# One half's 31-wide convolution as a short Fourier transform on TensorE, and two weight buffers that move into memory the mixer leaves

## The chip, the cores and the metric

The kernel runs on one core of one Trainium2 chip. A core has five engines that each take their own instructions in order: TensorE (PE in the profile; its weight loads are PEld), VectorE (DVE), ScalarE (ACT), GpSimd (POOL) and SyncE (SP), which here only issues DMA transfers. The metric is the device time of one execution in microseconds (us); lower is better. A difference of less than about 0.3% (3.8 us) can't be told from no change by a measurement of this kernel.

## The reference

One layer, on `x` of 1024 tokens by 1024 channels in float32. Its mixer projects the normed tokens, runs an RWKV-7 recurrence on 512 channels and a causal convolution on the other 512, and projects both back; a gated feed-forward network with a 3-wide causal convolution follows. Cut to what matters here:

```python
h = rms_norm(x, norm_pre_mix)
p = h @ w_in
u, q = p[..., :1024], p[..., 1024:]
...                                        # q: RWKV-7 recurrence, group norm, gate -> rwkv_out
c = u[..., :512] * sigmoid(u[..., 512:])
c = causal_dwconv(c, cconv_w, cconv_b)     # 31 taps for each of 512 channels
c = silu(layer_norm(c, cln_g, cln_b))
mix = concatenate([rwkv_out, c], -1) @ w_out
x = x + rms_norm(mix, norm_post_mix)
h = rms_norm(x, norm_pre_ffn)
hid = causal_dwconv(h @ ffn_up, ffn_conv_w, ffn_conv_b)          # 3 taps
gate, up = hid[..., :2816], hid[..., 2816:]
f = (gelu(gate) * up) @ ffn_down
return x + rms_norm(f, norm_post_ffn)
```

## The kernel before

The tokens are worked on in two halves of 512 (h = 0 and 1); the recurrence divides each half into two quarters of 256 (q0 to q3), and a quarter into chunks. Each large product is three matmuls on fp32r operands: a float32 operand is split into a rounded high part and a low remainder (`split`: ACT casts the high part, DVE or POOL subtracts), and high by high, low by high and high by low are added in PSUM. TensorE works through: the projections of half 0, then of half 1; the recurrences of q0 to q2; `w_out(0)`, the output projection of half 0 (768 matmuls of 256 columns in four rounds, with banks `pb`); the norm between mixer and feed-forward for half 0 (`norm_ffn`, tiles `row` and `pt`, which reads the mixer's result back from `mixd` in DRAM); then EARLY = 9 of the feed-forward's up-projections for half 0 (432 matmuls of 512 columns), among which the recurrence of q3 runs; then `w_out(1)`, and the rest of the feed-forward.

The convolution stands beside all this. `conv(h, i)` is, for one block of 128 channels, one ACT instruction (tap 0 and the bias, L428) and 30 DVE SCALAR_TENSOR_TENSOR instructions on 128x512 (L431), accumulating in the PSUM bank `pc`, the last into a tile `co`. `conv_norm(h)` then transposes 128 tokens at a time on TensorE (tiles `co` into `pc`), takes the layer norm over channels on DVE, transposes back (`t2` into `pc`), and applies Silu with gain and bias on ACT (L452). For half 1 the `co` tiles are operands of `w_out(1)`.

Instructions are put in order, per engine, by a scheduler that simulates the program with priorities. A piece of code runs in a "stream" whose number is its priority (`PRIO`, smaller goes first: rwkv 1000, top 100000, norm 200000, conv 300000, proj 400000). `w_out` and the early feed-forward pairs are in "proj", `norm_ffn` of half 0 in "top". `issue_after` gates `conv(1, 0)` and `conv(1, 1)` behind the last Silu of half 0, `conv(1, 2)` behind a mark of q3.

Names used below: `m` are the split operands of `w_out(0)` (L167 is `split`'s subtraction); `mixr` holds the recurrence's results, finished in L774 and L775; `inverses` (L606 and L608, tiles `sub` and `dw`) inverts the small triangular matrices of a quarter by 14 pairs of dependent DVE instructions; `f` are the split operands of the feed-forward (L294); weights are loaded as `wr` and split to `wh` and `wl`, from pool `wp` (3 raw buffers, 2 pairs) and `wq` (2 raw, 1 pair).

## Time and profile before

| | |
|---|---|
| median of 3 runs | 1254.13 us (1252.01 to 1255.34) |
| the profiled execution | 1257.58 us, its span 1255.8 us |
| granted TensorE clock, mean | 0.985 |
| busy: PE, DVE, ACT, POOL | 1210.4, 899.8, 729.1, 507.1 us |

The profiled execution is 3.45 us above the median, and 1.8 us of it lie outside the span. In the profile a line such as L431 is a line of the kernel; `out<-in` gives the tiles by name; "x" counts instructions. A window's columns are the busy us of each engine, then the clock that TensorE was granted (1.00 is full speed), the share of the DMA engines' time, and GB/s. A duration that a record of a matmul shows contains its latency: how fast matmuls follow each other is read from a run of many of them. In the chain of waits, each row is what the engine work was released by, followed back in time.

### The profile page before, as it was taken

How to read it: one execution, taken by the hardware profiler on the slowest of the kernel's cores; microseconds unless marked ns; L12 is line 12 of the kernel's file. 1: busy time of each engine (PE TensorE's matmuls, PEld its weight loads, DVE VectorE, ACT ScalarE, POOL GpSimd, SP SyncE). 2: the span in 40 equal slices, each digit the busy share in tenths (PEclk: the TensorE clock that was granted, in tenths of full speed). 3: DMA queues.
4: the chain of work that ended last, by engine and by line, in shares of the span. 5: the costliest groups of instructions: out<-in, count | busy, mean ns of one | idle time of the engine just before them, and what ended most of it. 6: DMA issues, size and time to landing. Idle time of an engine off the chain costs nothing.

```text
span 1255.8 us, 22979 instructions
## 1 busy us (share of the span) xinstructions
PE 1210.4 (96%) x8424; PEld 988.9 (79%) x8424; DVE 899.8 (72%) x1558; ACT 729.1 (58%) x1515; POOL 507.1 (40%) x447
## 2 busy tenths in 40 slices
PE   5999999999999998999999999999999999999997
PEld 4767777787778876778889888888888888888885
DVE  5285998898669989998640555666656679479667
ACT  7563564565955676466762576876555566554451
POOL 4343330001103331344563399998888850000002
PEclk9999998999999989999999999999999999999999
DMA  7644442333343353222364798894322335336413
GB/s 243 177 131 137 129 135 64 97 128 119 114 128 91 97 178 110 75 80 85 104 186 118 271 323 293 298 315 153 82 74 81 101 134 166 95 117 219 134 52 134
DMA packets 102912, 180.97 MB, mean 144 GB/s; under 512 B 14896, under 2 KB 21424, under 8 KB 102800
## 3 DMA queue, kind: packets, MB, share of 16 engines
q1 hardware_dynamic: 102800, 179.51, 45.6%
q8 instruction: 66, 1.08, 0.4%
q14 instruction: 46, 0.38, 0.1%
HBM read 138.44 MB, written 41.03 MB: 143 GB/s over the span
## 4 chain that ended last, share of the span: by engine, by line
PE 62%; DVE 6%; ACT 2%; issue 1%; DMA 1%; POOL 1%; POOLq 0%; DVEq 0%; ACTq 0%
PE pb L140 27%; PE xs L140 16%; PE pe L140 14%; PE Y L140 2%; PE pc L140 2%; DVE pc L431 2%; DMA pt<-mixd 1%; PE pc L155 1%; PE pe L155 0%; DVE x L1120 0%; DVE m L167 0%; DVE sub L606 0%; DVE nrow L1136 0%; DVE dw L608 0%; DVE t L797 0%
## 5 line engine op out<-in xcount | busy, mean ns | idle before, releaser
L167 POOL TENSOR_TENSOR wl<-wr,wh 128x512 fp32r<-128x512 f32 (+1 forms) x175 | 230.0, 1316 | 219.4 <-ACT wh L167 191.3
L140 PE MATMUL pb<-h,wh 128*128 128x512 f32 (+3 forms) x720 | 230.1, 399 | 2.5 <-ACT wh L167 1.0
L167 ACT CAST wh<-wr 128x512 fp32r<-128x512 f32 (+1 forms) x214 | 131.4, 615 | 131.8 <-issue 42.3
L140 PE MATMUL pb<-f,wh 128*128 128x512 f32 x648 | 205.0, 397 | 2.7 <-ACT wh L167 1.7
L431 DVE SCALAR_TENSOR_TENSOR pc<-c,params,pc 128x512 f32<-128x512 f32 x232 | 174.2, 751 | 8.7 <-ACT pc L428 4.7
L140 PEld LDWEIGHTS pb<-h,wh 128*128 128x128 f32 (+2 forms) x720 | 132.1, 189 | 35.4 <-ACT wh L167 2.7
L140 PE MATMUL pb<-h,wl 128*128 128x512 f32 (+3 forms) x360 | 146.8, 408 | 2.3 <-POOL wl L167 2.1
L140 PEld LDWEIGHTS pb<-f,wh 128*128 128x128 f32 x648 | 121.8, 190 | 28.8 <-ACT wh L167 2.1
L140 PE MATMUL pb<-f,wl 128*128 128x512 f32 x324 | 129.2, 399 | 0.9 <-POOL wl L167 0.9
L162 POOL TENSOR_TENSOR ss<-var,mhalf 128x1 f32<-128x1 f32 x16 | 11.4, 716 | 223.8 <-DVE var L161 223.0
L1076 POOL TENSOR_TENSOR b<-b,b 128x512 f32<-128x512 f32 x72 | 93.3, 1298 | 1.9 <-DMA wr<-ffn_up 0.5
L140 PEld LDWEIGHTS pb<-h,wl 128*128 128x128 f32 (+2 forms) x360 | 67.8, 188 | 20.5 <-POOL wl L167 4.0
L140 PE MATMUL xs<-f,wh 128*128 128x512 f32 x240 | 74.2, 390 | 0.4 <-DVE act L973 0.4
L167 POOL TENSOR_TENSOR wl<-b,wh 128x512 fp32r<-128x512 f32 x48 | 66.6, 1388 | 16.9 <-ACT wh L167 14.9
L140 PEld LDWEIGHTS pb<-f,wl 128*128 128x128 f32 x324 | 61.7, 190 | 14.8 <-POOL wl L167 1.7
L167 ACT CAST wh<-b 128x512 fp32r<-128x512 f32 x48 | 29.7, 618 | 60.0 <-PE pb L140 20.5
L140 PE MATMUL pe<-f,wh 128*128 128x512 f32 x208 | 64.1, 389 | 0.0
L721 POOL TENSOR_TENSOR XG<-r,GE 64x256 f32<-64x256 f32 x30 | 20.5, 683 | 89.3 <-DVE r L740 84.5
L140 PEld LDWEIGHTS xs<-f,wh 128*128 128x128 f32 x240 | 44.9, 188 | 10.0 <-DVE act L973 0.8
L192 ACT CAST wh<-wr 128x512 fp32r<-128x512 f32 (+2 forms) x44 | 26.5, 604 | 44.4 <-PE pb L140 31.2
L167 ACT CAST a<-act 128x512 fp32r<-128x512 f32 x50 | 30.0, 620 | 33.6 <-PE Y L140 19.1
L167 ACT CAST w<-wr 128x512 fp32r<-128x512 f32 x38 | 23.4, 622 | 40.7 <-PE Y L140 20.0
(419 smaller groups left out, 2952.3 us busy)
## 6 DMA issues: line engine op xcount, KB each, us to landing
wr<-ffn_up SPq DMA_DIRECT2D x99, 256.0 KB, 3.2
wr<-w_in SPq DMA_DIRECT2D x80, 256.0 KB, 2.9
b<-ffn_up SPq DMA_DIRECT2D x52, 256.0 KB, 2.7
b<-ffn_down SPq DMA_DIRECT2D x44, 256.0 KB, 4.5
sums<-b SPq DMA_DIRECT2D x44, 256.0 KB, 4.2
wr<-sums SPq DMA_DIRECT2D x44, 256.0 KB, 2.8
lows<-wl SPq DMA_DIRECT2D x40, 256.0 KB, 3.3
wl<-lows SPq DMA_DIRECT2D x40, 256.0 KB, 2.7
```

Of the source, the lines that this page charges most:

```text
L140: return self.nc.tensor.matmul(out, lhsT, rhs, start=start, stop=stop, skip_group_check=skip)
L155: self.nc.tensor.transpose(out, in_, self.con("ident")[:n, :n])
L162: self.nc.gpsimd.tensor_tensor(out, v[:, :n], self.mhalf[:, :n], ALU.pow)
L167: return self.nc.scalar.copy(hi, src), eng.tensor_tensor(lo, src, hi.bitcast(F32), ALU.subtract)
L192: self.nc.scalar.copy(hi, raw)
L431: nc.vector.scalar_tensor_tensor(out, c[:, j:j + HALF], w(j), acc, ALU.mult, ALU.add)
L721: nc.gpsimd.tensor_tensor(x[64:128], R[64:128, gs], w.GE[64:128, c, gs].unsqueeze(2).broadcast_to([64, 4, CH]), ALU.mult)
L1076: sub = lambda o, x, y, op=ALU.subtract: self.nc.gpsimd.tensor_tensor(o, x, y, op)
```

## The change

For half 1, `conv` and `conv_norm` are replaced by `waves`. The 512 tokens, with the 30 before them, are taken in six blocks of SPAN = 116 tokens, of which the last FRESH = 86 are kept (the last block overlaps the fifth). For each block: four transposes put the tokens on partitions (116 tokens by 512 channels, bank `pc`); ACT and DVE split that into `xy`; three matmuls by constant cosines and sines (`wave`) give the spectrum; DVE multiplies it by the taps' spectrum (`tapf`; three multiplications, the last two with halves of the partitions exchanged, and an addition); ACT and DVE split the product into `xy` again; three matmuls transform back to 86 tokens, a last row of `xy` adding the bias; layer norm over the channels on DVE and POOL; four transposes back, and four ACT instructions with gain and bias into `co`. After the sixth block four ACT instructions apply Silu. All blocks use the one bank `pc` and the one `xy`, one after the other. `conv_setup`, once, loads the constants and the taps, splits the constants, and computes `tapf` by two float32 matmuls. The gates of half 1's convolution are gone; `waves(1)` stands in the program behind `w_out(0)`, in stream "proj" ("wave" in PRIO is not used).

The pool `wq` is opened in `setup_ffn`, where the mixer's memory has been given back, and not in `setup`.

Line numbers move: `mm` is L140 before and L162 after, `transpose` L155 and L177, `split`'s subtraction L167 and L189, the inverses L606/L608 and L701/L703, `mixr` L774/L775 and L869/L870.

```diff
+HALO = CONV_W - 1
+SPAN = 116
+FRESH = SPAN - HALO
+NFREQ = SPAN // 2 + 1
...
-        "mixr": 1, "co": 4, "po": 1, "c": 4, "t2": 2}
+        "mixr": 1, "co": 4, "po": 1, "c": 4, "t2": 2, "t3": 2}
...
+def waves():
+    angle = 2 * np.pi / SPAN * (np.arange(SPAN)[:, None] * np.arange(NFREQ)[None, :] % SPAN)
+    cos, sin = np.cos(angle), np.sin(angle)
+    w = np.zeros((P, 3 * P + FRESH), np.float64)
+    w[:SPAN, 0:NFREQ] = cos
+    w[:SPAN, 64:64 + NFREQ] = sin
+    times = np.where(np.arange(NFREQ) % (SPAN // 2) == 0, 1, 2)[:, None] / (2 * SPAN)
+    w[0:NFREQ, P:P + FRESH] = (times * cos.T)[:, :FRESH]
+    w[64:64 + NFREQ, P:P + FRESH] = (times * sin.T)[:, :FRESH]
+    w[P - 1, P:P + FRESH] = 1
+    o = P + FRESH
+    w[:CONV_W, o:o + NFREQ] = w[:CONV_W, o + 64:o + 64 + NFREQ] = cos[:CONV_W]
+    o += P
+    w[:CONV_W, o:o + NFREQ] = -sin[:CONV_W]
+    w[:CONV_W, o + 64:o + 64 + NFREQ] = sin[:CONV_W]
+    return w.astype(np.float32)
+
...
         pool = next(self.homes[tag]) or self.wp
-        bufs = {self.wp: (RAW, PAIRS), self.wq: (MORE_RAW, MORE_PAIRS)}[pool][tag != "wr"]
+        bufs = ((RAW, PAIRS) if pool is self.wp else (MORE_RAW, MORE_PAIRS))[tag != "wr"]
         return pool.tile(shape, dt, tag=tag, bufs=bufs, name=self.nm(tag))
...
         self.wp = ctx.enter_context(tc.tile_pool(name="wp", bufs=1))
-        self.wq = ctx.enter_context(tc.tile_pool(name="wq", bufs=1))
         self.hp = ctx.enter_context(tc.tile_pool(name="hp", bufs=2 * KT))
...
         self.ccarry = cp.tile([P, 4, 32], F32, name="ccarry")[:, :, :CONV_W - 1]
+        self.wave = cp.tile([P, 2, P + FRESH], F32R, name="wave")
+        self.tapf = cp.tile([P, 2, D_CONV], F32, name="tapf")
+        self.xy = cp.tile([P, 2, D_CONV], F32R, name="xy")
...
+
+    def conv_setup(self):
+
+        nc = self.nc
+        raw, tap = (self.tl("ca", [P, 512]) for _ in range(2))
+        nc.sync.dma_start(raw[:, :3 * P + FRESH], self.a["waves"])
+        nc.sync.dma_start(tap[:CONV_W + 1], self.a["taps"])
+        n = P + FRESH
+        nc.scalar.copy(self.wave[:, 0], raw[:, :n])
+        nc.vector.tensor_tensor(self.wave[:, 1], raw[:, :n], self.wave[:, 0].bitcast(F32), ALU.subtract)
+        for e in range(2):
+            ps = self.bank("pc")
+            self.mm(ps, raw[:CONV_W, n + e * P:n + (e + 1) * P], tap[:CONV_W])
+            nc.scalar.copy(self.tapf[:, e], ps)
+        hi, lo = (self.xy[0:32, e] for e in range(2))
+        nc.scalar.copy(hi, tap[0:32])
+        nc.vector.tensor_tensor(lo, tap[0:32], hi.bitcast(F32), ALU.subtract)
+        for e, t in enumerate((hi, lo)):
+            nc.sync.dma_start(self.xy[P - 1:P, e].bitcast(F32), t[CONV_W:].bitcast(F32))
+
+    def waves(self, st):
+
+        nc = self.nc
+        co = [self.tl("co", [P, HALF]) for _ in range(4)]
+        hi, lo = self.xy[:, 0], self.xy[:, 1]
+        n = P - 1
+
+        def product(w, k):
+            ps = self.bank("pc")
+            m = w.shape[2]
+            for i, (a, b) in enumerate(((0, hi), (0, lo), (1, hi))):
+                self.mm(ps[:m], w[:k, a], b[:k], start=i == 0, stop=i == 2)
+            return ps
+
+        def two(k, src):
+            nc.scalar.copy(hi[:k], src[:k])
+            nc.vector.tensor_tensor(lo[:k], src[:k], hi[:k].bitcast(F32), ALU.subtract)
+
+        for b in range(6):
+            t0 = min(b * FRESH, HALF - FRESH)
+            ps = self.bank("pc")
+            for i in range(4):
+                self.transpose(ps[:SPAN, i * P:(i + 1) * P], st["c", i][:, t0:t0 + SPAN])
+            two(SPAN, ps)
+            ps = product(self.wave[:, :, :P], SPAN)
+            y, swap = (self.tl("t3", [P, D_CONV]) for _ in range(2))
+            nc.vector.tensor_tensor(y[:n], ps[:n], self.tapf[:n, 0], ALU.mult)
+            nc.vector.tensor_tensor(swap[0:64], ps[64:128], self.tapf[64:128, 1], ALU.mult)
+            nc.vector.tensor_tensor(swap[64:n], ps[0:n - 64], self.tapf[0:n - 64, 1], ALU.mult)
+            nc.vector.tensor_tensor(y[:n], y[:n], swap[:n], ALU.add)
+            two(n, y)
+            ps = product(self.wave[:, :, P:], P)[:FRESH]
+            bs = self.small.tile([P, 6], F32, tag="cs", name=self.nm("bs"))[:FRESH]
+            nc.vector.bn_stats(bs, ps)
+            mv = self.small.tile([P, 4], F32, tag="cs", name=self.nm("mv"))[:FRESH]
+            nc.vector.bn_aggr(mv[:, 0:2], bs)
+            nc.vector.tensor_scalar(mv[:, 3:4], mv[:, 1:2], 1.0, LN_EPS, ALU.mult, ALU.add)
+            nc.gpsimd.tensor_tensor(mv[:, 2:3], mv[:, 3:4], self.mhalf[:FRESH, 0:1], ALU.pow)
+            xn = self.tl("t3", [P, D_CONV])[:FRESH]
+            nc.vector.tensor_scalar(xn, ps, mv[:, 0:1], mv[:, 2:3], ALU.subtract, ALU.mult)
+            ps = self.bank("pc")
+            for i in range(4):
+                self.transpose(ps[:, i * P:i * P + FRESH], xn[:, i * P:(i + 1) * P], FRESH)
+            for i in range(4):
+                nc.scalar.activation(co[i][:, t0:t0 + FRESH], ps[:, i * P:i * P + FRESH], AF.Identity,
+                                     bias=self.par("cln_b", i), scale=self.par("cln_g", i))
+            yield
+        for i in range(4):
+            nc.scalar.activation(co[i], co[i], AF.Silu)
+            st["co", i] = co[i]
...
         pool = lambda name, bufs=1: ctx.enter_context(tc.tile_pool(name=name, bufs=bufs))
+        self.wq = pool("wq")
         cp = pool("fconst")
...
+        def waves(h):
+
+            with self.stream("proj"):
+                list(self.waves(sts[h]))
+
...
         conv_norm(0)
+        with self.stream("conv"):
+            self.conv_setup()
         project(1, hs, "u0 u1 u2 u3")
...
         step(self.bonus, 2)
-        conv(1, 0, sts[0]["normed"])
-        conv(1, 1, sts[0]["normed"])
         with self.stream("proj"):
             self.w_out(0, mixes[0], [sts[0]["co", i] for i in range(4)])
+        waves(1)
         mixes[1] = self.tl("mixr", [P, 4, HALF])
...
                                ("pb",), dg))
-        conv(1, 2, W[3].mark)
-        conv(1, 3)
-        conv_norm(1)
         with self.stream("proj"):
...
     out["consts"] = constants()
+    out["waves"] = waves()
+    out["taps"] = np.concatenate([f("cconv_w")[0].reshape(CONV_W, D_CONV), f("cconv_b")[0].reshape(1, D_CONV)])
     out["post_mix"] = f("norm_post_mix")
```

Three places in the order of instructions, as built. In a row stand line, operation, output, inputs and shape; a number behind a name is the tile's, and "x3" merges equal rows.

VectorE, at the end of q2's inverses and the first splits `m` for `w_out(0)`. Before, the convolution's L431 stands between nearly all of the steps:

```order
L431 SCALAR_TENSOR_TENSOR pc_703_4615<-c_526_3352,params_78,pc_703_4615 128x512
L606 TENSOR_TENSOR sub_628_4031<-dw_103 128x54
L167 TENSOR_TENSOR m_707_4681<-mixr_338_2009,m_706_4680 128x512
L167 TENSOR_TENSOR m_709_4683<-mixr_338_2009,m_708_4682 128x512
L431 SCALAR_TENSOR_TENSOR pc_703_4615<-c_526_3352,params_78,pc_703_4615 128x512
L608 TENSOR_TENSOR dw_103<-dw_103,sub_628_4031 128x9x6
L382 TENSOR_SCALAR gd_699_4602<-gd_699_4602 96x512
L167 TENSOR_TENSOR m_711_4685<-mixr_338_2009,m_710_4684 128x512
L480 TENSOR_SCALAR kk_640_4066<-pe_641_4073 128x512
L431 SCALAR_TENSOR_TENSOR pc_703_4615<-c_526_3352,params_78,pc_703_4615 128x512
L606 TENSOR_TENSOR sub_629_4034<-dw_103 128x56
```

After, on the same engine and place:

```order
L703 TENSOR_TENSOR dw_100<-dw_100,sub_639_4068 128x2x13
L870 TENSOR_TENSOR mixr_338_2009<-mixr_338_2009,pe_617_3976 128x4x128
L701 TENSOR_TENSOR sub_640_4071<-dw_100 128x14
L703 TENSOR_TENSOR dw_100<-dw_100,sub_640_4071 128x14
L711 STREAM_TRANSPOSE dw_100<-dw_100 64x16x32
L715 STREAM_TRANSPOSE l8_626_4022<-dw_100 64x16x32 x2
L189 TENSOR_TENSOR m_707_4631<-mixr_338_2009,m_706_4630 128x512
L525 TENSOR_TENSOR t3_794_5211<-pc_793_5207,tapf_126 127x512
L526 TENSOR_TENSOR t3_795_5212<-pc_793_5207,tapf_126 64x512
L527 TENSOR_TENSOR t3_795_5212<-pc_793_5207,tapf_126 63x512
```

All of q2's inverses and their last transposes have moved ahead of the first `m`, and a block's spectrum (L525 to L527) stands where L431 stood.

TensorE, at the first matmuls of the feed-forward (`pb` from `f`). Before:

```order
L155 MATMUL xs0_100<-const_79,v_662_4403 64x128 x2
L140 MATMUL pe_831_5506<-pt_645_4218,const_79 128x512
L140 MATMUL pe_832_5509<-pt_655_4318,const_79 128x512
L140 MATMUL pb_899_6087<-kk_856_5937,row_888_6028 128x128
L140 MATMUL pb_899_6087<-kk_856_5937,row_892_6044 128x128
L140 MATMUL pb_899_6087<-kk_856_5937,row_888_6028 128x128
L140 MATMUL pb_899_6087<-kk_856_5937,row_892_6044 128x128
L155 MATMUL xs1_101<-const_79,v_677_4484 64x128 x2
L140 MATMUL pb_929_6255<-f_868_5976,wh_931_6258 128x512
```

After:

```order
L162 MATMUL xs1_98<-r_901_6027,ck_867_5629 64x64
L162 MATMUL Y_102<-r_901_6027,ca_851_5504 64x64
L162 MATMUL xs1_98<-r_901_6027,ck_867_5629 64x64
L162 MATMUL Y_102<-r_901_6027,ca_851_5504 64x64
L162 MATMUL pc_823_5339<-xy_127,wave_125 86x512 x3
L162 MATMUL pb_959_6295<-f_926_6174,wh_961_6298 128x512
L162 MATMUL pb_959_6295<-f_927_6175,wh_961_6298 128x512
```

The last matmuls of a half's norm are no longer next to the feed-forward's first: chunk matmuls of the recurrence and the fourth block's inverse transform stand directly ahead of it.

TensorE, at the last matmuls for half 1's convolution, amid the 432 of the early feed-forward. Before, the last transposes back (`t2` into `pc`) stand behind 396 of them:

```order
L140 MATMUL pb_1061_6955<-f_875_5983,wh_1063_6958 128x512
L140 MATMUL pb_1061_6955<-f_874_5982,wl_1064_6959 128x512
L155 MATMUL pc_927_6245<-const_79,t2_926_6243 128x128 x4
L140 MATMUL pb_1061_6955<-f_876_5984,wh_1066_6976 128x512
L140 MATMUL pb_1061_6955<-f_877_5985,wh_1066_6976 128x512
```

After, the last block's transposes back (`t3` into `pc`) stand behind 193:

```order
L162 MATMUL pb_1016_6599<-f_940_6188,wl_1022_6621 128x512
L162 MATMUL pb_1025_6645<-f_926_6174,wh_1027_6648 128x512
L177 MATMUL pc_845_5431<-const_76,t3_844_5429 128x86 x4
L162 MATMUL pb_1025_6645<-f_927_6175,wh_1027_6648 128x512
L162 MATMUL pb_1025_6645<-f_926_6174,wl_1028_6649 128x512
```

They have moved forward by about four of the nine feed-forward pairs, and none of the convolution's work is left near `w_out(1)`.

2 lines of the change are left out of this document (1 added, 1 removed).

## The prediction

> **What bounds the kernel now.** I read the page first: engines, chain, groups.
>
> ```profile
> span 1255.8 us, 22979 instructions
> PE 1210.4 (96%) x8424; PEld 988.9 (79%) x8424; DVE 899.8 (72%) x1558; ACT 729.1 (58%) x1515; POOL 507.1 (40%) x447
> PE 62%; DVE 6%; ACT 2%; issue 1%; DMA 1%; POOL 1%; POOLq 0%; DVEq 0%; ACTq 0%
> L431 DVE SCALAR_TENSOR_TENSOR pc<-c,params,pc 128x512 f32<-128x512 f32 x232 | 174.2, 751 | 8.7 <-ACT pc L428 4.7
> ```
>
> TensorE bounds most of the span. The removed work (half of L431) is on VectorE, which the chain visits for 6%. So the change pays only where VectorE stops TensorE. The busy time by stage tells where:
>
> ```profile
> 390.00:411.00 21.00, 20.76 (x155) 19.53 (x154) 21.00 (x43) 10.68 (x25) 6.54 (x5) 0.92 0.31 88
> 411.00:457.00 46.00, 44.61 (x724) 41.19 (x724) 43.37 (x69) 33.85 (x76) 16.59 (x15) 1.00 0.43 119
> 457.00:500.00 43.00, 36.50 (x449) 27.53 (x442) 36.24 (x87) 29.17 (x76) 10.60 (x14) 0.92 0.43 144
> 500.00:560.00 60.00, 59.57 (x700) 47.56 (x701) 56.30 (x93) 33.44 (x69) 24.51 (x20) 0.97 0.26 76
> 560.00:633.00 73.00, 72.91 (x534) 58.82 (x532) 56.57 (x92) 48.28 (x102) 33.87 (x28) 1.00 0.31 93
> 633.00:641.00 8.00, 5.38 (x19) 4.05 (x19) 5.30 (x6) 6.13 (x12) 5.04 (x5) 0.79 0.49 146
> 641.00:700.00 59.00, 58.64 (x438) 56.17 (x437) 8.22 (x13) 19.22 (x53) 26.15 (x21) 1.00 0.50 145
> 700.00:1250.00 550.00, 546.27 (x2425) 451.78 (x2423) 375.84 (x600) 320.66 (x657) 287.86 (x228) 1.00 0.53 170
> ```
>
> From 390 to 457 both are full (VectorE 21.0 of 21.0, 43.4 of 46.0). A busy PE is not PE at its peak there, since latencies of small dependent matmuls count. From 641 on TensorE is dense and VectorE has nothing of the convolution: that part stays. Its order is the same in both kernels from `w_out(1)` on, so the whole result is decided by when `w_out(1)` begins. The chain of waits gives the stage borders:
>
> ```profile
> 388.85 0.60 DVE mixr L775
> 413.67 0.18 DVE dw L608
> 470.06 4.17 DMA pt<-mixd
> 500.38 10.71 PE pb L140 x46
> 636.39 15.67 PE pb L140 x106
> 652.05 11.52 PE xs L140 x96
> 773.37 10.88 PE pb L140 x48
> ```
>
> And from TensorE's and VectorE's timelines:
>
> ```profile
> 389.50 1.09 PE L155 MATMUL pe<-const,l 128*128 128x128 f32 x8 [2.19 <-DVE mixr L775]
> 390.35 0.36 PE L140 MATMUL pb<-wh,m 128*128 128x256 f32 x1
> 456.54 0.28 PE L140 MATMUL pb<-wh,m 128*128 128x256 f32 x1
> 634.74 0.73 PE L140 MATMUL pb<-f,wh 128*128 128x512 f32 x2 [1.70 <-ACT wh L167]
> 636.39 0.50 PE L140 MATMUL pb<-f,wl 128*128 128x512 f32 x1 [0.92 <-POOL wl L167]
> 379.15 0.17 DVE L606 TENSOR_TENSOR sub<-dw 128x14 f32<-128x14 f32 x1
> 493.76 0.18 DVE L606 TENSOR_TENSOR sub<-dw 128x14 f32<-128x14 f32 x1
> 508.19 0.17 DVE L608 TENSOR_TENSOR dw<-dw,sub 128x14 f32<-128x14 f32 x1
> ```
>
> Stage A, `w_out(0)`, runs from 390.4 to 456.8: 66.4 us. Stage B, the norm, ends with the first feed-forward matmul at 500.4: 43.6. Stage C, early feed-forward and q3, ends with the first matmul of `w_out(1)`. Its first 96 matmuls of 256 columns end at 652.05 and take 11.52 us by the next 96, so it begins at 640.5: C is 140.1. Behind it lie 615.3 us to the end. A 512-column matmul streams at 10.88/48 = 0.227 us, a 256-column one at 0.120.
>
> The convolution slows the chain in A, where by VectorE's groups it takes half of the engine's time (first row, 390 to 457; the second is of stage B):
>
> ```profile
> L431 DVE SCALAR_TENSOR_TENSOR pc<-c,params,pc 128x512 f32<-128x512 f32 x44 | 32.9, 748 | 0.4
> L555 DVE TENSOR_TENSOR l<-pe,const 128x256 f32<-128x256 f32 x8 | 3.3, 416 | 0.1
> ```
>
> Therefore q2's inverses take 379.15 to 413.85 between L431s, 34.7 us; q3's, with few of them, 493.76 to 508.36, 14.6.
>
> **The change, part by part.** The `pc` tile view prices the old instructions:
>
> ```profile
> L431 DVE SCALAR_TENSOR_TENSOR pc<-c,params,pc x232: 723/756/757, 134.5 to 583.2; 128x512 f32<-128x512 f32 x116
> L155 PE MATMUL pc<-const,t x32: 270/273/328, 318.6 to 627.0; 128*128 128x128 f32 x32
> L452 ACT ACTIVATE co<-pc,params x32: 447/458/466, 322.1 to 631.1; 128x128 f32<-128x128 f32 x32
> L428 ACT ACTIVATE pc<-c,params x8: 772/780/785, 133.7 to 543.1; 128x512 f32<-128x512 f32 x8
> L447 DVE TENSOR_SCALAR t<-pc,mv x8: 800/810/811, 315.4 to 624.0; 128x512 f32<-128x512 f32 x8
> 391.71 1.28 DVE L167 TENSOR_TENSOR m<-mixr,m 128x512 fp32r<-128x512 f32 x2
> 496.78 1.88 PE L140 MATMUL pe<-pt,const 128*128 128x512 f32 x4
> 511.02 2.20 PE L140 MATMUL pe<-dw,l 32*32 32x16 f32 x128
> ```
>
> *VectorE* loses 120 x 0.75 = 90 us of L431 and 4 x 1.9 of norm (two passes over 512 of at most L447's 0.81, two tiny ones) = 7. Each of six blocks adds two splits (2 x 0.64), three multiplications from PSUM and one addition (between a split's 0.64 and L447's 0.81: 3.0), statistics and norm (1.8): 6.1, together 36. Net -61 us.
>
> *ScalarE* loses 4 x 0.78 and 16 x 0.46 = 10.4; gains per block two casts (bounded by L428's 0.78; about 0.62) and four of at most 0.46: 3.0, and four final Silu of about 0.7: +21. Net +10, on an engine that is 58% busy; no wait of it is on the path except at the tail below.
>
> *TensorE* gains 36 matmuls of 512 columns, 8.2 us, and loses 32 transposes of 128 columns for 48 shorter ones, +1.0 (eight transposes take 1.09 us in the 389.50 row, 0.11 to 0.12 each behind the first; the 273 ns is latency; 86 columns I take at 0.08). Two float32 512-column products cost 1.88 by the 496.78 row (four pieces there). Sum +11, and all of it is on the engine that bounds. This is the price against the gain.
>
> *Set-up* (two loads and two row copies on SP's queue, six splits and copies) comes at about 240 us, among loads that wait for free buffers in the same way. SP would hold the following weight loads if a `ca` buffer came late; bounds 0 to some 3 us (a load's landing), I take 0: whatever TensorE loses ahead of 389 is covered, since it waits there 2.19 us for `mixr`, a VectorE result. The 2.5 us that set-up and the first block put on TensorE before `w_out(0)` are hidden there too.
>
> *The weight buffers.* The first two loads into `wq` stand amid `w_out(1)`'s in both orders, and after the change they have no wait on the mixer. Cost 0; if they had, one late weight costs about what the tail shows now, 1.7 + 0.9 us, plus the clock.
>
> *Where the work moves, by the order.* Priced with the rates above, and the small ones by the pace of their streams (2.20/128 us a record in the 511.02 row, up to 0.06 for 64 columns by estimate), TensorE's own work is, before and after: A 58.6 and 71.0; B 26.4 and 30.4; C 123.0 and 115.2. The freed VectorE lets the scheduler pull q2's chunk products and scores into A (+8.6 of the 12.4; blocks are the rest), and q3's inverses and their matmuls into B.
>
> Start of A: ahead of the first `m`, VectorE sheds about fifteen L431 (10 us), but now does all the rest of q2's inverses and three transposes there (about 9). So `m` is ready when it was: start 390.
>
> A: 71.0 of work, 1.7 for the half-clock stretch (below), and 2.3 of waits, where 66.4 - 58.6 - 1.7 = 6.1 are now. VectorE sheds 33 us of L431 here and takes on some 20 (a block and a half, q3's scores), so its waits shorten; the blocks bring their own chain through one bank, so they don't vanish. 75.0, +8.6.
>
> B: a chain, not an engine, sets it (PE work 26.4 of 43.6): results to DRAM and back (4.17 for a tile), `row`, `pt`, `f`. VectorE is busy 36.2 of 43 now. By the order q3's scores, which L555 stands for, leave it for A (L555 3.3, L556, L564 and L597 with it; some 11 us), and two blocks (12 us) and the rest of q3's inverses (up to 14.6 less what waits there, some 6 by the 0.18 rows) enter. Above, that makes 43.6 + 12 = 55.6 if the blocks stand wholly on the chain; below, 40 if what leaves is on the chain and what enters fits into waits such as the 4.17. I take 45.6, +2.0, near to now, since what leaves and what enters differ by only 7 us and the norm's own `row` steps keep their places.
>
> C: 115.2 of work. Of the 17.1 us above the work now, 2.6 are the two gaps at 634.74 and 636.39, where TensorE waits for weights that ACT and POOL split late behind the convolution's norm, and 3.4 two half-clock stretches. The tail's two go: the last block now ends half a stage earlier. The other 11.1 are the mixing of small dependent matmuls with feed-forward; a third of those matmuls left, and the last 48.6 us are feed-forward alone, so I take 6. 115.2 + 1.7 + 6 = 122.9, -17.2. What is late next at the tail: nothing of the mixer; weights, at their present pace.
>
> Sum: +8.6 + 2.0 - 17.2 = -6.6. Against the profiled 1257.58 that is 1251.0; against the median, 3.45 lower, 1247.5.
>
> **The clock.** Three stretches ran at half speed:
>
> ```profile
> 391.20:394.60 3.40, 3.40 (x11) 2.37 (x12) 3.40 (x8) 3.40 (x8) 0.00 (x0) 0.50 0.00 0
> 459.50:466.30 6.80, 6.66 (x52) 3.71 (x52) 2.99 (x7) 4.68 (x15) 1.40 (x2) 0.50 0.90 287
> 637.00:640.40 3.40, 3.40 (x10) 2.63 (x9) 1.30 (x2) 1.98 (x3) 2.27 (x2) 0.50 0.61 176
> ```
>
> Each 3.4 us cost 1.7. The last follows gaps of 1.70 and 0.92 us, so removing the tail's stall also removes 1.7. The Trainium skill (TensorE: Matmul & The Clock Gate, "HAM oscillation") has the rule that idle gaps of TensorE over about 3.4 us matter; by it the tail's short gaps cost no clock, and the sum would be -4.9. The trace disagrees: its gaps are shorter, and the clock fell. The same page (Part 4) says that transposes on TensorE don't count as busy for the gate; with more of them and of small matmuls in A and B, one more half-clock stretch would follow, and the sum by it would be -4.9 too. No run here shows that alone.
>
> **Rivals.**
> 1. *The norm becomes VectorE's* (slower). Blocks and q3's inverses stand between the norm's own `row` and `f` instructions, in order. For: 36.2 of 43 us busy there already, and the first feed-forward matmul has a block's inverse transform ahead of it on TensorE, so it waits for that block's VectorE work. Against: q3's scores leave. At B = 56, the upper end, the sum is +3.8, the point from which it is slower; with half the inverses besides (63), +11. About 1259.
> 2. *No change.* The pulled-forward work saves nothing since it was dense where it was: waits stay 6.1 in A, and 9 in C: -6.6 + 3.8 + 3 = about 0: 1254. For: VectorE's share of the chain is 6%. Against: 34.7 us for inverses that take 14.6.
> 3. *More gain.* With VectorE free, A is as dense as its work (72.7), B is 40, C 120: 6.3 - 3.6 - 20.1 = -17: about 1237. For: TensorE's work in the three rises 8.6 us, and 42 us of them are not its work now (66.4 + 43.6 + 140.1 less 208.0).
> 4. *The buffers' move delays the feed-forward's weights*: +4. Against: no wait in the order.
>
> **How the numbers follow.** The forecast has 0.50, its own range 1242.5 to 1252.5; 0.39 of it is faster by over 0.3% (3.8 us; below 1250.4), 0.11 within. Rival 1: 0.20, slower. Rival 2: 0.15, of which 0.12 is within and 0.03 slower. Rival 3: 0.13, faster. Rival 4: 0.02, within, as it takes most of the gain back. Faster 0.55, same 0.25, slower 0.20. The range 1238 to 1259 leaves out nearly half of rival 1 and most of rival 3, 2 in 10.
>
> **What would show it.** Right: L431 x116; `w_out(0)` from 390 to about 465; the first feed-forward matmul near 511; first matmul of `w_out(1)` near 634 with no gap on `wh` and `wl` ahead and no half clock; 615 us behind it. Wrong: B over 55 us with VectorE over 95% busy and TensorE idle on `f` or `pc` (rival 1); `w_out(1)` at 640 with C at 128 (rival 2); `w_out(0)` ending by 463 and B at 40 (rival 3); a `wr` from `ffn_up` that lands late in `w_out(1)` (rival 4). The sum fails most easily in B, the stage with no bound from its own work.

## The result, and the profile after

The changed kernel takes 1270.37 us (median of 5 runs, 1267.52 to 1273.3) against 1254.65 before (5 runs): ratio 1.0135, 95% interval 1.0122 to 1.0147. It is 16 us slower, where 6.6 us faster had been forecast. The page of its profile:

```profile
span 1270.8 us, 23041 instructions
PE 1222.7 (96%) x8480; PEld 999.5 (79%) x8480; DVE 846.3 (67%) x1484; ACT 734.3 (58%) x1535; POOL 504.5 (40%) x449
L455 DVE SCALAR_TENSOR_TENSOR pc<-c,params,pc 128x512 f32<-128x512 f32 x116 | 87.1, 751 | 3.4 <-ACT pc L452 0.9
```

The change did what it says: half of the convolution's instructions are gone (x116), and VectorE is busy 53.5 us less. TensorE is busy 12.3 us more. The three stages, with borders read as in the prediction, and two stretches inside the second (windows: PE, PEld, DVE, ACT, POOL busy, then the clock):

```profile
391.50:474.70 83.20, 81.38 (x1096) 73.12 (x1095) 51.85 (x90) 52.66 (x121) 27.78 (x26) 1.00 0.34 104
474.70:527.30 52.60, 43.38 (x746) 35.70 (x745) 41.40 (x101) 37.69 (x93) 9.38 (x14) 0.77 0.29 94
527.30:654.50 127.20, 123.19 (x766) 98.59 (x765) 73.08 (x110) 73.73 (x157) 59.20 (x48) 1.00 0.31 94
487.10:490.50 3.40, 3.40 (x49) 2.62 (x49) 3.29 (x8) 2.43 (x7) 0.13 (x1) 0.50 0.38 140
493.90:514.40 20.50, 16.06 (x310) 14.41 (x311) 15.56 (x36) 11.77 (x29) 4.87 (x7) 0.50 0.38 130
```

| | start of A | A, `w_out(0)` | B, norm | C, early feed-forward | from `w_out(1)` on |
|---|---|---|---|---|---|
| before | 390.4 | 66.4 | 43.6 | 140.1 | 615.3 |
| forecast | 390 | 75.0 | 45.6 | 122.9 | 615.3 |
| after | 391.5 | 83.2 | 52.6 | 127.2 | 616.3 |

C did shrink, by 12.9 us, and the tail's stall is gone. A and B grew by 16.8 and 9.0 us, about twice what C gave back. In B the trace shows how TensorE is held up. TensorE's timeline (a bracket is the idle time ahead of a row, and what ended it):

```profile
486.64 1.32 PE L162 MATMUL pc<-xy,wave 116*128 116x512 f32 x3
492.89 0.46 PE L162 MATMUL pc<-xy,wave 128*86 128x512 f32 x1 [1.66 <-ACT xy L514]
496.62 1.16 PE L162 MATMUL pc<-xy,wave 128*86 128x512 f32 x2 [3.27 <-DVE xy L515]
504.87 2.93 PE L162 MATMUL pb<-kk,row 128*128 128x128 f32 x12 [1.72 <-DVE mv L535]
...
526.51 0.94 PE L162 MATMUL pc<-xy,wave 128*86 128x512 f32 x3
527.29 0.62 PE L162 MATMUL pb<-f,wh 128*128 128x512 f32 x2
...
654.45 1.72 PE L162 MATMUL pb<-wm,l 128*128 128x256 f32 x13
```

and VectorE's, at the longest of these waits:

```profile
491.45 0.68 DVE L528 TENSOR_TENSOR t<-t,t 127x512 f32<-127x512 f32 x1
...
493.15 0.75 DVE L982 SCALAR_TENSOR_TENSOR row<-pt,nr,row 128x512 f32<-128x512 f32 x1 [0.88 <-DMA pt<-mixd]
493.82 0.17 DVE L703 TENSOR_TENSOR dw<-dw,sub 128x14 f32<-128x14 f32 x1
495.21 0.75 DVE L982 SCALAR_TENSOR_TENSOR row<-pt,nr,row 128x512 f32<-128x512 f32 x1 [1.22 <-DMA pt<-mixd]
495.88 0.68 DVE L515 TENSOR_TENSOR xy<-t,xy 127x512 fp32r<-127x512 f32 x1
```

A block's inverse transform waits on TensorE, 1.66 and 3.27 us, for the split L514 and L515 of its spectrum. The low part's L515 had its operands early: L514 was done at 492.8. But it is queued behind two `row` steps of the norm, for which VectorE waits 0.88 and 1.22 us on DMA transfers. So the block waits for the norm's DMA, and everything behind the block in TensorE's queue, the norm's matmuls of `kk` and `row` among it, waits for the block: the in-order queues hold each other up. Those matmuls later wait 1.72 us more, put down to a tiny step of a block's norm (L535) that ran among the norm's own. TensorE's clock is at half for 20.5 us meanwhile (493.9 to 514.4).

### The profile page after: what moved, and what is told of

Read it like the earlier page. It is cut to its first block, busy times and chain, and to the rows that moved or that the text cites. A ratio compares the mean times of both kernels' runs of the same rounds, so it can differ in the third digit from the quotient of the medians.

```text
span 1270.8 us, 23041 instructions
## 1 busy us (share of the span) xinstructions
PE 1222.7 (96%) x8480; PEld 999.5 (79%) x8480; DVE 846.3 (67%) x1484; ACT 734.3 (58%) x1535; POOL 504.5 (40%) x449
## 4 chain that ended last, share of the span: by engine, by line
PE 50%; DVE 1%; DMA 0%; POOL 0%; issue 0%; DVEq 0%; POOLq 0%; ACT 0%
PE pb L162 19%; PE xs L162 15%; PE pe L162 12%; PE Y L162 2%; PE pc L162 2%; DVE x L1216 0%; DVE nrow L1232 0%; DMA mixd<-t 0%; PE pc L177 0%; PE Y L177 0%; POOL ss L184 0%; DVE t L892 0%; DVE act L1069 0%; DVEq L1579 0%; POOLq L1579 0%
## 5 line engine op out<-in xcount | busy, mean ns | idle before, releaser
L189 POOL TENSOR_TENSOR wl<-wr,wh 128x512 fp32r<-128x512 f32 (+1 forms) x175 | 227.9, 1304 | 228.3 <-ACT wh L189 185.0
L162 PE MATMUL pb<-h,wh 128*128 128x512 f32 (+3 forms) x720 | 230.4, 399 | 2.5 <-ACT wh L189 1.0
L162 PE MATMUL pb<-f,wh 128*128 128x512 f32 x648 | 202.1, 392 | 3.0 <-ACT wh L189 1.5
L189 ACT CAST wh<-wr 128x512 fp32r<-128x512 f32 (+1 forms) x214 | 131.3, 615 | 126.7 <-issue 41.4
L162 PEld LDWEIGHTS pb<-h,wh 128*128 128x128 f32 (+2 forms) x720 | 131.9, 189 | 35.9 <-ACT wh L189 2.7
L162 PE MATMUL pb<-h,wl 128*128 128x512 f32 (+3 forms) x360 | 146.8, 408 | 2.3 <-POOL wl L189 2.2
L162 PEld LDWEIGHTS pb<-f,wh 128*128 128x128 f32 x648 | 121.0, 188 | 29.3 <-ACT wh L189 2.3
L162 PE MATMUL pb<-f,wl 128*128 128x512 f32 x324 | 127.5, 394 | 0.6 <-POOL wl L189 0.6
L455 DVE SCALAR_TENSOR_TENSOR pc<-c,params,pc 128x512 f32<-128x512 f32 x116 | 87.1, 751 | 3.4 <-ACT pc L452 0.9
L162 PEld LDWEIGHTS pb<-h,wl 128*128 128x128 f32 (+2 forms) x360 | 67.7, 188 | 20.9 <-POOL wl L189 4.0
L162 PE MATMUL xs<-f,wh 128*128 128x512 f32 x240 | 74.2, 390 | 1.4 <-DVE act L1069 1.4
L189 POOL TENSOR_TENSOR wl<-b,wh 128x512 fp32r<-128x512 f32 x48 | 65.5, 1366 | 19.6 <-ACT wh L189 17.9
L162 PEld LDWEIGHTS pb<-f,wl 128*128 128x128 f32 x324 | 60.8, 188 | 14.1 <-POOL wl L189 1.4
L189 ACT CAST wh<-b 128x512 fp32r<-128x512 f32 x48 | 29.7, 618 | 59.8 <-PE pb L162 21.2
L162 PE MATMUL pe<-f,wh 128*128 128x512 f32 x208 | 64.1, 389 | 0.0
L162 PEld LDWEIGHTS xs<-f,wh 128*128 128x128 f32 x240 | 44.9, 188 | 11.1 <-DVE act L1069 1.8
L1015 DVE SCALAR_TENSOR_TENSOR pt<-pb,params,pt 128x511 f32<-128x511 f32 (+1 forms) x36 | 26.9, 747 | 34.8 <-ACT ecarry L1008 34.2
L189 ACT CAST a<-act 128x512 fp32r<-128x512 f32 x50 | 30.0, 619 | 33.6 <-PE Y L162 19.1
```

The source lines that it names most:

```text
L162: return self.nc.tensor.matmul(out, lhsT, rhs, start=start, stop=stop, skip_group_check=skip)
L189: return self.nc.scalar.copy(hi, src), eng.tensor_tensor(lo, src, hi.bitcast(F32), ALU.subtract)
L455: nc.vector.scalar_tensor_tensor(out, c[:, j:j + HALF], w(j), acc, ALU.mult, ALU.add)
L1015: nc.vector.scalar_tensor_tensor(acc[:, o:], ps[:, :HALF - o], w(j), acc[:, o:], ALU.mult, ALU.add)
```

## The experiments

Each is compared with runs of the kernel before on the same chip. "Rows" are the TensorE rows of the recurrence that the order puts into A, B and C (before: 262, 208, 420; after: 376, 354, 164). Stages are those of one profiled run each. e1's and those of the kernel before have the same matmuls, within the few records that a trace lacks, and differ by up to 2.1 us (C), so a smaller difference of one stage says little by itself. e2, e7, e9 and e13 to e18 leave out work of half 1's convolution and compute something else there.

| | median us | ratio, 95% interval | start, A, B, C, rest |
|---|---|---|---|
| e1 buffers only | 1253.37 | 0.9992, 0.9981 to 1.0004 | 389.9, 65.7, 42.3, 138.0, 615.5 |
| e2 two taps | 1258.68 | 1.0040, 1.0025 to 1.0055 | 387.7, 78.5, 42.7, 132.5, 615.4 |
| e3 blocks behind norm | 1274.24 | 1.0154, 1.0128 to 1.0180 | 390.1, 76.5, 44.2, 136.0, 626.3 |
| e4 36 matmuls more | 1259.58 | 1.0041, 1.0027 to 1.0055 | 390.3, 66.2, 41.5, 144.2, 615.6 |
| e5 before, `w_out(0)` first | 1274.04 | 1.0157, 1.0121 to 1.0192 | 390.6, 56.9, 61.3, 146.9, 616.7 |
| e6 after, `w_out(0)` first | 1279.21 | 1.0197, 1.0167 to 1.0226 | 391.5, 63.3, 60.2, 144.2, 616.8 |
| e7 two taps, `w_out(0)` first | 1270.75 | 1.0130, 1.0094 to 1.0166 | 386.5, 63.0, 51.6, 148.8, 615.4 |
| e8 after, blocks first too | 1279.85 | 1.0204, 1.0173 to 1.0236 | 390.5, 64.2, 64.9, 139.0, 618.5 |
| e9 two taps, recurrence held | 1254.24 | 1.0001, 0.9986 to 1.0016 | 386.8, 69.4, 42.6, 137.7, 615.6 |
| e10 after, recurrence held | 1271.38 | 1.0130, 1.0095 to 1.0164 | 391.4, 71.2, 53.5, 138.5, 616.7 |
| e11 e10, five blocks behind the norm | 1274.48 | 1.0158, 1.0119 to 1.0196 | 390.5, 69.3, 46.5, 147.8, 618.4 |
| e12 after, 24 matmuls fewer | 1271.38 | 1.0136, 1.0111 to 1.0160 | 391.4, 87.4, 51.2, 123.4, 615.4 |
| e13 after, no product | 1270.51 | 1.0128, 1.0107 to 1.0149 | 389.7, 82.2, 45.2, 132.6, 618.4 |
| e14 e9 and set-up | 1257.32 | 1.0034, 1.0021 to 1.0046 | 388.2, 68.4, 42.3, 139.4, 616.8 |
| e15 e14 and TensorE's work | 1261.36 | 1.0058, 1.0042 to 1.0074 | 389.4, 68.8, 43.6, 142.9, 616.8 |
| e16 e14 and the steps | 1271.63 | 1.0133, 1.0108 to 1.0158 | 388.3, 76.9, 46.9, 141.0, 616.0 |
| e17 e14, work and steps | 1267.83 | 1.0107, 1.0079 to 1.0135 | 388.3, 77.9, 44.9, 138.2, 616.3 |
| e18 e12 and e13 together | 1263.26 | 1.0059, 1.0041 to 1.0077 | 389.6, 79.2, 48.1, 129.7, 615.3 |

**The parts of the change, one at a time.** The buffers alone:

```diff
-        self.wq = ctx.enter_context(tc.tile_pool(name="wq", bufs=1))    # setup
+        self.wq = pool("wq")                                            # setup_ffn
```

> The kernel before with only the pool wq moved into setup_ffn. Theory 1 (work: each microsecond that the blocks and the tap spectra add to TensorE is paid, wherever they stand) and theory 2 (place: the blocks cost because they and the chunks pulled forward stand in w_out(0) and in the norm): no change, 1254 to 1255. Rival: the buffers' move itself delays loads, then 3 us or more of the 16 are here.

No change; this part of the prediction holds. The relief of VectorE alone:

```diff
-        for j in range(1, CONV_W):
+        for j in range(first, CONV_W):          # first = CONV_W - 1 for half 1
```

> The kernel before, with half 1's convolution cut to its first and last tap (116 of 120 VectorE instructions of it left out, so it computes another convolution there); its norm and transposes stay, and nothing is added. It is the relief of VectorE alone. By the prediction's reasoning (waits in w_out(0), mixing among the early feed-forward and the tail's stall come from VectorE's queue): 15 us or more faster, 1235 to 1240. Theory 1: TensorE was idle only 11 us in these stages and at half clock for 17 us; VectorE is behind a part of that, so 4 to 8 us faster, 1247 to 1251. Theory 2 says the same of the relief as long as the chunks it pulls forward do no harm; if they do (the order is looser and the norm gets longer), no gain or a loss, 1253 to 1262.

With 87 us less for VectorE and nothing more for any engine, the kernel is slower, by 0.40%, where the prediction's reasoning asks for 15 us or more the other way; theory 2's 1253 to 1262 holds. This was the run that overturned the forecast. Its stages:

```profile
387.70:466.20 78.50, 76.07 (x1047) 68.67 (x1044) 42.10 (x73) 49.59 (x114) 25.06 (x23) 1.00 0.38 114
466.20:508.90 42.70, 31.05 (x567) 26.06 (x565) 36.04 (x93) 28.19 (x68) 10.70 (x14) 0.92 0.34 115
508.90:641.40 132.50, 129.45 (x952) 103.63 (x950) 64.26 (x100) 81.56 (x171) 62.30 (x49) 0.99 0.31 90
```

A is 12 us longer, since the scheduler pulls chunks forward (rows 360, 274, 260). C gives back 7.6, and the norm keeps its 43 us with TensorE less busy in it (31.05 us; 36.5 of 43 before). Blocks out of the norm, and their TensorE work as idle repeats in the kernel before:

```diff
-        waves(1)                                # behind w_out(0)
+        with tc.issue_after(self.mark_lo.ins):  # behind norm_ffn(0)
+            waves(1)
```

> The changed kernel, with the six blocks gated behind half 0's norm, so that all of them stand among the early feed-forward. Theory 1: their matmuls cost the same there, 1264 to 1268 (only the norm's extra idle time of some 3 us comes back). Theory 2: the norm falls back to 44 us, its half-clock stretch of 20 us goes, w_out(0) ends earlier; 1250 to 1257.

B fell to 44.2, as theory 2 says, but the time didn't: the last block came so late that `w_out(1)` waited for it (5.70 us at 672.41, for the split of a `co`), and the rest grew by 11. Both theories missed. Inconclusive on the work.

```diff
+                for _ in range(extra if first else 0):      # 2 for the nine early pairs
+                    self.mm(ps[:m], wh[:, kk], hi)
```

> The kernel before, with two idle repeats of the first matmul of each up-projection in the nine early pairs: 36 matmuls of 512 columns more (the number that the blocks add), and nothing else. Theory 1: 36 x 0.227 = 8.2 us slower, 1262 to 1263. If TensorE has slack there that they fill (what the prediction called mixing), less: 1256 to 1259.

36 matmuls cost 5.1 us (interval 3.4 to 6.9), less than their 8.2 at 0.227, and between the two expectations. Added work is paid for the most part.

**Giving the recurrence another place.** e2 suggested a third theory, that the norm is a chain of fixed length in which chunk products are free. Four runs put `w_out(0)` ahead of the recurrence:

```diff
+PRIO = {"out": 500, ...}
-        with self.stream("proj"):
+        with self.stream("out"):
             self.w_out(0, ...)
```

> The kernel before, with w_out(0) in a stream of its own, ahead of the recurrence (number 500, rwkv has 1000): q2's chunk products leave w_out(0) for the norm and the early feed-forward (262 matmul rows of the recurrence in w_out(0) before, 105 here). Theory 3, formed from the runs so far: the norm is a chain of some 43 us whatever TensorE does in it, so chunk products are free there and are paid in w_out(0) and among the feed-forward; freeing VectorE only made the scheduler pull them into w_out(0). By it w_out(0) falls to about 59, the norm stays at 44, the early feed-forward grows to about 146: 1250 to 1255. Rival (theory 1: work is work wherever it stands): no change, 1254.

> The changed kernel, with w_out(0) in the same stream ahead of the recurrence (376 matmul rows of the recurrence in w_out(0) after the change, 164 here). Theory 3: w_out(0) about 64 instead of 83, the norm about 48 (it keeps blocks), the early feed-forward about 141; 1255 to 1261, so most of the 16 us come back. Theory 1: the blocks' work is paid all the same: 1264 or more.

> The kernel before with half 1's convolution cut to two taps (116 VectorE instructions left out), and w_out(0) ahead of the recurrence. Theory 3: the relief is worth something only so: w_out(0) 61, norm 43, early feed-forward 141; 1246 to 1251, against 1258.7 with the relief alone. Theory 1: TensorE's work is that of the kernel before, so 1252 to 1255. If the relief itself did the harm and not the pulled-forward chunks: 1257 or more.

> The changed kernel, with w_out(0) and the six blocks in the stream ahead of the recurrence: the blocks end after 96 of the 432 early matmuls, and 34 of their TensorE rows stand in the norm. Theory 3: w_out(0) about 64, and the norm as after or longer, since more blocks' chains stand on TensorE's queue in it (50 to 55): 1257 to 1264. Theory 1: 1264 or more.

Theory 3 missed all four, by 16 to 20 us. Theory 1's "1264 or more" held for e6 and e8, its 1254 for e5 did not, so moving the recurrence costs by itself. A shrank as expected (56.9 in e5), but the norm is no free room. Its stages in e5, the kernel before with only this edit:

```profile
390.60:447.50 56.90, 55.66 (x588) 52.70 (x586) 51.84 (x88) 27.53 (x61) 21.72 (x18) 0.98 0.36 102
447.50:508.80 61.30, 49.05 (x660) 39.43 (x659) 43.03 (x91) 41.30 (x105) 9.28 (x13) 0.72 0.38 123
508.80:655.70 146.90, 142.10 (x1309) 111.59 (x1310) 124.52 (x200) 88.74 (x183) 63.83 (x54) 0.99 0.28 84
```

With the chunks in it B is 61.3 us at a clock of 0.72. The third theory fell: B does not get shorter with less in it, but longer with more.

So the next runs held how much of the recurrence stands in each stage. Putting only the first two of `w_out(0)`'s four rounds ahead gives rows 266, 208, 420, nearly those of the kernel before:

```diff
+            with self.stream("out") if h == 0 and ch in (0, 1) else ExitStack():
+                round(ch)
```

> The kernel before with half 1's convolution cut to two taps (116 VectorE instructions left out) and only the first two of w_out(0)'s four rounds ahead of the recurrence. That puts as much of the recurrence into each stage as the kernel before has (matmul rows of it in w_out(0), norm, early feed-forward: 266, 208, 420; before 262, 208, 420; with the relief alone 360, 274, 260). Theory 4, from the runs so far: the norm's chain has a floor of some 42 us; less TensorE work than fits into it is idle time there, more (or work in long dependent chains at half clock) lengthens it, and the kernel before happens to stand at the best filling. By it the relief at this filling is a small gain: 1247 to 1253 (tail and waits in w_out(0)), against 1258.7 for the relief with chunks pulled forward. Rival: VectorE's instructions do no harm where they were, and the loss of the relief had another cause: 1255 or more.

```profile
386.80:456.20 69.40, 66.45 (x863) 60.97 (x860) 34.69 (x51) 44.36 (x100) 23.64 (x21) 1.00 0.39 109
456.20:498.80 42.60, 35.88 (x455) 27.18 (x453) 36.00 (x87) 29.39 (x76) 9.98 (x14) 0.96 0.44 146
498.80:636.50 137.70, 135.36 (x1245) 107.53 (x1246) 70.96 (x128) 87.39 (x177) 61.47 (x51) 1.00 0.29 87
```

Theory 4's gain did not come; the time is that of the kernel before, 1.0001. VectorE is busy 34.7 us in A, where it was 64.4 of 67 from 390 to 457, and q2's inverses end at 388.95 instead of 413.85. `w_out(0)` starts 3.6 us earlier, since TensorE's wait of 2.19 us for `mixr` is gone, but A is 3.0 us longer and ends where it did (456.2; 456.8 before). A wait as long has come up on another tile (first row TensorE, the others VectorE):

```profile
393.79 0.39 PE L140 MATMUL pb<-wh,m 128*128 128x256 f32 x1 [2.21 <-DVE gd L365]
388.79 0.16 DVE L608 TENSOR_TENSOR dw<-dw,sub 128x14 f32<-128x14 f32 x1
389.58 1.13 DVE L616 STREAM_TRANSPOSE dw<-dw 64x512 f32<-64x512 f32 x1
390.73 2.10 DVE L620 STREAM_TRANSPOSE l<-dw 64x512 f32<-64x512 f32 x2
392.99 0.74 DVE L365 SCALAR_TENSOR_TENSOR gd<-pb,params,gd 96x511 f32<-96x511 f32 x1
```

L365 empties a bank `pb`, and is queued behind the transposes that follow the inverses. The tail's two gaps are gone too, but C's 137.7 is no shorter than the 138.0 of e1, which has the same gaps (1.70 and 0.92 us) and a whole convolution. So the relief moved waits and brought no time. Two limits: e9 holds the recurrence's share of each stage, not the order itself, and the first two rounds put ahead without the cut were not run, so it is not shown that this edit costs nothing alone.

> The changed kernel with only the first two of w_out(0)'s rounds ahead of the recurrence: the recurrence is distributed as before (266, 208, 420 matmul rows), and the blocks stand as after (a block and a half in w_out(0), two in the norm, the rest behind it). Theory 4: the pulled-forward chunks' share comes back, the blocks' own work (8 to 9 us) and their stalls in the norm (6 to 9 us) stay: 1261 to 1267. If the chunks pulled forward are not part of the loss: 1270.

> As the last, with only the first block free to run in w_out(0) and the other five gated behind half 0's norm, so that no block stands in the norm and the last ends behind 374 of the 432 early matmuls. Theory 4: the norm is back at 42 to 44, w_out(0) at 67 to 69, the early feed-forward at 143 to 147 with five blocks' work: 1256 to 1261, so that only the blocks' TensorE work is left of the loss. If the blocks' stalls on TensorE cost as much among the feed-forward as in the norm: 1264 or more.

Theory 4 missed both; the other expectation, 1270 for e10 and 1264 or more for e11, held in both. Holding the recurrence shortens A by 12 us and lengthens C by 11. With one block early and five behind the norm (`next(blocks)` once, the others gated), B comes down to 46.5, and C goes up to 147.8, 10 us over e9's with the same matmuls of recurrence and feed-forward. Of these 10, five blocks' 30 matmuls are 6.8 at 0.227. The blocks' cost moves with them.

**Work or chains.** The changed kernel with fewer matmuls, with a shorter chain, and with both:

```diff
-            for i, (a, b) in enumerate(((0, hi), (0, lo), (1, hi))):      # e12, e18
-                self.mm(ps[:m], w[:k, a], b[:k], start=i == 0, stop=i == 2)
+            self.mm(ps[:m], w[:k, 0], hi[:k])
...
-            nc.vector.tensor_tensor(y[:n], ps[:n], self.tapf[:n, 0], ALU.mult)   # e13, e18: all four gone
-            two(n, y)
+            two(n, ps)
```

> The changed kernel with one matmul in place of three in each of the blocks' transforms (high part by high part only, so the convolution is less exact): 24 matmuls of 512 columns, 5.4 us of TensorE, are gone; VectorE's and ScalarE's steps stay. Theory 1 (the loss is TensorE's added work): 1264 to 1266. Theory 5 (the loss is the blocks' chains, in which TensorE's in-order queue stands still): no change, 1269 to 1271.

> The changed kernel without the multiplication by the taps' spectrum (three multiplications and one addition on VectorE, 3 us of each block's chain, are left out, so that no convolution is computed); all of TensorE's work stays. Theory 1: no change, 1268 to 1271. Theory 5: the chain is shorter by six times 3 us, of which the two to four blocks that TensorE waits for come back: 1260 to 1265.

> The changed kernel with both cuts: one matmul of three, and no multiplication by the taps' spectrum. The recurrence then stands as in the first two-tap run (360, 274, 260 matmul rows in the three stages; that was 1258.7). Theory 1: 1264 to 1266. Theory 5: 1260 to 1266, as chains are shorter and fewer of them stand in the norm. If neither work nor chain length matters, only that blocks stand in TensorE's queue at all: 1268 to 1271.

Neither edit alone moved the time, as theory 5 had it for e12 and theory 1 for e13; neither theory has both. The two together took the ratio from 1.0135 to 1.0059, within theory 5's range. In e13 the norm did fall, to 45.2, and C and the rest rose by 7.5. The order is made anew for each kernel, and gives one stage what another saves; effects do not add. The other way round, on top of e9, the change was built up piece by piece:

```diff
+            self.conv_setup()                   # e14 to e17
+            self.work(sts[1])                   # e15, e17: 36 matmuls, 16 transposes into pc, constant operands
+            self.steps(sts[1])                  # e16, e17: casts, subtractions, products, norms in SBUF
```

> The kernel of the two-tap run with the held distribution (1254.2), and conv_setup (loads, splits, two float32 matmuls) besides, whose results are not used, with wq moved to make room. Prediction's pricing: hidden ahead of w_out(0), 1254. Theory 1: its 1.9 us of TensorE and some 2 us by which w_out(0) begins later in all kernels that have it: 1256 to 1258.

> The last kernel, with the blocks' TensorE work besides, without their chains: six times three 512-column matmuls by the cosines and three by the inverse, on constant operands, and 16 transposes, into the bank pc, with nobody waiting for the results; no VectorE or ScalarE step of a block. TensorE then has as much work as in the changed kernel. Theory 1: 1264 to 1269. Theory 5: work without chains fills TensorE's idle time in the norm, 1256 to 1261, and the rest of the loss up to 1270 is the chains.

> The set-up run (1257.3) and the blocks' VectorE and ScalarE steps besides, on other data in memory and with no TensorE work: six times two casts, two subtractions, three multiplications and one addition, and for two blocks the norm (the other four norms stand for those of the old code, which stays). Results unused. Theory 5 (the loss beyond set-up and work is the waits between the engines): 1256 to 1259, since VectorE and ScalarE are not the bound. Rival: these steps hold up the norm's and the recurrence's on their in-order engines: 1262 or more.

> The work-alone run (1261.4) with the same steps besides: as much work on every engine as in the changed kernel, but the blocks' matmuls don't wait for the steps, nor the steps for them. Theory 5: 1261 to 1264, and the 7 to 9 us up to the changed kernel are the waits between matmuls and steps. Rival (load on VectorE and ScalarE): 1267 or more.

Against the kernel before: relief 0.0%, with set-up 0.34%, with TensorE's work 0.58%, with work and steps 1.07%, the change 1.35%. In e15 the norm takes up the extra matmuls (TensorE busy 40.9 of 43.6, clock 1.00, where e9 has 35.9), much as theory 5 had it, though 1261.36 lies just above its range:

```profile
389.40:458.20 68.80, 68.02 (x875) 62.37 (x873) 29.70 (x47) 43.98 (x99) 24.11 (x21) 1.00 0.39 113
458.20:501.80 43.60, 40.90 (x491) 31.13 (x489) 35.34 (x90) 29.98 (x76) 8.50 (x13) 1.00 0.41 136
501.80:644.70 142.90, 137.35 (x1254) 110.47 (x1249) 75.97 (x125) 87.86 (x180) 63.11 (x52) 0.98 0.29 85
```

But e16 and e17 went against theory 5, and for its rival: the steps alone, with no matmul added, cost 1.0133 against 1.0034, some 12 us. Five rows of VectorE's timeline in `w_out(0)` of e16, and one of TensorE's:

```profile
399.21 0.67 DVE L512 TENSOR_TENSOR t<-t,tapf 64x512 f32<-64x512 f32 x1
399.89 1.68 DVE L513 TENSOR_TENSOR t<-t,tapf 52x512 f32<-52x512 f32 x1
401.60 0.75 DVE L455 SCALAR_TENSOR_TENSOR co<-c,params,pc 128x512 f32<-128x512 f32 x1
402.27 0.69 DVE L189 TENSOR_TENSOR m<-co,m 128x512 fp32r<-128x512 f32 x1
...
408.33 0.69 DVE L506 TENSOR_TENSOR t<-c,t 116x512 f32<-116x512 f32 x1 [2.31 <-ACT t L505]
...
403.01 0.80 PE L162 MATMUL pb<-wh,m 128*128 128x256 f32 x2 [1.24 <-DVE m L189]
```

The split L189 of an operand of `w_out(0)` stands behind two steps, L512 and L513, and TensorE waits 1.24 us for it. At L506, VectorE itself stands still for 2.31 us until ScalarE has made a step's cast. A in windows, again:

```profile
388.30:465.20 76.90, 69.99 (x862) 64.16 (x860) 62.20 (x87) 52.16 (x119) 27.45 (x22) 0.93 0.34 97
```

VectorE is busy 62.2 us, no more than with the old convolution, and A is 8.5 us longer than in e14; TensorE is idle 6.9 us in it (1.9 in e14), and its clock is 0.93. But the scheduler put the steps elsewhere than in the changed kernel: in e16 and e17 all 43 of VectorE's steps stand ahead of B, 34 of them in A; in the changed kernel 2 stand ahead of A, 18 in A, 16 in B and 24 in C. The two runs show what such steps can cost in `w_out(0)`, not what they cost where the change has them.

## Why the prediction was wrong

**The step that failed first** is that the prediction took what its priced work for TensorE left over in a stage for time that a freer VectorE gives back: waits in A, mixing in C. In A it had 6.1 us of waits. In the windows of the kernel before TensorE is idle for 1.6 us there, and for 11.3 in the three stages:

```profile
390.40:456.80 66.40, 64.77 (x860) 60.12 (x860) 63.77 (x108) 43.96 (x99) 23.13 (x20) 0.97 0.39 109
456.80:500.40 43.60, 36.72 (x454) 27.78 (x453) 36.84 (x89) 29.77 (x78) 10.60 (x14) 0.92 0.43 142
500.40:640.50 140.10, 137.34 (x1246) 109.89 (x1247) 117.76 (x188) 86.94 (x179) 63.34 (x51) 0.98 0.30 88
```

The three stages held 42.1 us that were not its work, and the sum took 15.2 of them back. Of the 42.1, 11.3 were idle, and the half clock (17.0 us of it, from 391.2, 459.5, 514.1 and 637.0) cost at most 8.5; in the other 22 TensorE was busy, longer than its streams' pace says. After the change TensorE is idle 15.1 us, not less, and busy 9.1 us longer. The 8.6 us of added work were paid; the 15.2 did not come back. That 9.1 is close to 8.6 is partly luck, as the stages' errors cancel (A's busy time +16.6 against 12.4 forecast, C's -14.2 against -7.8).

The belief in the 15.2 rested on a full VectorE in A, on L431's half of its time there, and on 34.7 us for inverses that took 14.6 elsewhere. e9 tests that: without the convolution, and with the recurrence's share of each stage held, A is 69.4 (66.4 before) and the time is the same. L431 itself filled gaps (0.4 us of idle time ahead of it in A). It did stand ahead of `mixr` (L431 at 387.57, L775 at 388.77), for which TensorE waited 2.19 us, but without it a wait of 2.21 us took that one's place; the inverses were slow and in time. The forecast's "its waits shorten" (A), "the other 11.1 are the mixing" (C), where I took 5 us back, and the sum's sign all stand on this step. Even the tail's two gaps, gone in e9, bought nothing that can be told from e1.

The stages miss the forecast by 21.6 us: A by 8.2, B by 7.0, C by 4.3, the start by 1.1 and the rest by 1.0. The chances were also added wrongly: by their own parts faster has 0.52 and slower 0.23, not 0.55 and 0.20.

**A, forecast 75.0, measured 83.2.** TensorE is idle 1.8 us there (forecast 2.3), at full clock; so the term that was mis-sized is the work, 71.0. It is 81.4. By the starts in the trace, the 288 matmuls of `w_out(0)` take 38.7 us with waits left out, 0.134 each where the stream's price is 0.120, and all the others in A take 42.7, where 36.4 was left for them. The price of the kernel before had the same fault (58.6, busy 64.8), and so had C's (115.2, busy 123.2). e2 shows the pull forward by itself (A 78.5). Held back in e10, it came out in C, so it is not what made the change slow.

**B, forecast 45.6, measured 52.6.** Rival 1 named the stage, and the wait of the first matmul for a block's VectorE work; its form was another. VectorE is busy 41.4 of 52.6 and was not the bound; in this trace the queues blocked each other, 1.66 + 3.27 + 1.72 us on TensorE, and 23.9 us are at half clock (6.8 before, in B's first part), which costs up to 8.5 us more than before. These waits are not needed for a long B: in e10 it is as long (53.5, with 15.7 us at half clock), and there TensorE waits for no split of a block. Against e14, which has the set-up and no blocks, e10 loses 11.2 us in B, 3.2 at the start and 2.8 in A. So with the recurrence held the loss stands in the norm. My range for B, up to 55.6, held; rival 1's chance of 0.20 was too low, as it needed no full engine, but its time, about 1259, was short too.

**C, forecast 122.9, measured 127.2**: -12.9, not -17.2. **Set-up**, forecast hidden, costs 0.34% (0.21 to 0.46) in e14: the 2.19 us wait that was to cover it had gone with the convolution (`w_out(0)` starts at 386.8 in e9, and at 388.2 with set-up). That is 1.4 us of some 4; where the others are lost is not shown.

**The buffers' move** costs nothing, as forecast. **TensorE's own work**, +11 in the forecast, is paid in part: 5.1 of 8.2 in e4, about 3 in e15 where the norm has room.

**What stays open.** Added one after the other, relief, set-up and work come to 0, some 4 and some 3 us; the order is made anew each time, so these are prices of this sequence of runs (e16, without the blocks' matmuls, is no faster than e17, with them). The other 9 to 10 come with the blocks' steps on VectorE and ScalarE, or with the waits between them and the matmuls. e16 and e17 show that such steps can cost this in in-order queues even where no matmul waits for them, but with the steps in A; in the changed kernel most stand in B and C, and e10 loses its time in B. How the 9 arise there is not settled: e17 comes within 4 us of it, and the intervals of e16, e17 and the change overlap. No version tried is faster than the kernel before; e1 is level with it.

## What to carry to other kernels

What a stage takes beyond its priced work is not all waiting: look at how long the bounding engine is idle before taking any of it back. An engine that is full beside the bound need not be a cost, and even a wait that is seen for it can come back on the next tile: thin its work, hold the rest of the order as far as possible, and see, before paying for its relief with work elsewhere. Here long independent instructions filled an in-order queue without loss in the end; short dependent steps between engines held up what was queued behind them, with no more busy time in the stage. Where a scheduler makes the order, one edit changes two things, and a run that holds the shares of the stages helps to separate them.
